# Seven products for a 2x2 block product in the attention's input projection, for sample tokens 512 to 2047

## The chip, the cores and the metric

The kernel runs on one core of a Trainium2 chip. The metric is the device time of one execution in microseconds (us). A core has these engines: PE does the matmuls (PEld, its weight loads, are listed apart), DVE, ACT and POOL work on rows of elements, and SP mostly starts DMA transfers. Each engine runs its own instructions in order and waits on semaphores for the others.

## The reference, cut to what matters

The program is one inference step of a two-layer network on 256 prompt tokens and 2048 sample tokens of 1024 channels. Layer 0 is a convolution branch. Layer 1 is an attention: the 2048 sample tokens form a grid of 32 rows and 64 columns, and each reads a neighbourhood of 8 rows and 16 columns and 512 cached context keys. The change lies in the projection that feeds it:

```
def na_project(h, w_in):                       # w_in: 1024 x 4096
    B, L, _ = h.shape
    q, k, v, z = jnp.split(h @ w_in, 4, axis=-1)
    heads = lambda t: t.reshape(B, L, N_HEADS, HEAD_DIM)    # 16 heads of 64
    return heads(q), heads(k), heads(v), z
...
        q, k, v, z = na_project(h, na_w_in[j])
        att = neighbourhood_attention(q, k, v, cache_k[:, j], cache_v[:, j], na_rpb[j])
        out = (att * jax.nn.silu(z)) @ na_w_out[j]
```

Here `h` is the normalized and modulated input of the layer. The inputs are float32. `na_rpb` is a table of biases per head, which the kernel turns into one masked bias table per head and kind of query row.

## The kernel before, in words

**Arithmetic.** Each float32 operand of a matmul is held as two rounded numbers, a high part (`h`, `hi`) and the remainder (`l`, `lo`). A product is three matmuls into the same PSUM bank: high by high, high by remainder, and remainder by high (lines L362 to L364 in `project`, L1009 to L1011 in `na_values`). The high part is a copy by ACT or a rounding by POOL (L107, `round_pool`); the remainder is a subtraction by POOL (L110, `rest_pool`) or DVE (L113, `rest_dve`). For weights, `halves` copies the high part on ACT (L354) and subtracts on POOL.

**Stages.** To some 720 us runs the convolution layer, whose order was written out by hand for all engines. Its output projection follows (`conv_out_pipeline`, `conv_out`), and the attention's input projection begins at 847 us beside its end. The attention over the sample tokens (`sa_...` tiles) begins near 1820 us, in an order written out for PE and DVE; the output projection (`o`) and the final norm end the program. Where no order is written by hand, a scheduler orders each engine's instructions from the program's order and from `high_priority` blocks. Most DMAs are issued by SP, in one queue, in order.

**The input projection.** It is done twice, for two sets of token blocks: A is the prompt, sample tokens 0 to 511 and 512 to 767; B is 768 to 1023, 1024 to 1535 and 1536 to 2047. For keys, queries and gate (`na_rest`, tiles `ni_...`), 128 output channels (one `ct` of eight) of one part (1 keys, 0 queries, 3 gate) stand as weights in PE, and a block of 256 or 512 tokens streams by, in eight steps of 128 input channels. A weight of 128 by 1024 (`nis_..._w`, or `nip_...` for A) is loaded and split for each of the 24 pairs of `ct` and part. For values (`na_values`, tiles `v_ps`), 128 tokens stand in PE and 256 channels of a weight (`wv_..._w`) stream by. A key is copied by ACT and its remainder is subtracted by DVE from PSUM; a query is scaled by ACT (L1056), then rounded and subtracted by POOL; the gate goes through a Silu on ACT (L1047). The results go to DRAM (`ks_d`, `qh_d`, `ql_d`, `zn_d`, `vs_d`) and are read back by the attention.

**Side work.** `weave(main, side, n)` steps through a main generator and, after each of its steps, `n` steps of a side generator. Beside values and rest of B are woven: the context keys (`context_keys`), the masked bias tables (`masked_bias`, DVE subtractions at L1106 into tiles `bm`, 48 stores to `bm_d`), the output weights times the gate (`gated_weights`, L1218), the context values, the prompt's own attention (`pa_...`), and its output projection (`po_...`). The last `ct` of B makes gate, keys, queries in this order, and between its last query products stand the scores of the attention's first two units (`begun`, lines L1616 and L1617). After them the attention transposes its probabilities on PE (L1649), splits them on ACT (L1658) and DVE (L113, tiles `sa_pt`), and multiplies them by the values (L1673, L1678).

The weave of set B reads:

```
side = itertools.chain(self.context_keys(), self.masked_bias())
self.weave(self.na_values(B, lambda: next(rest)), side, 2)
self.weave(itertools.islice(rest, 13), side, 3.6)
...
side = itertools.chain(self.gated_weights(), self.context_values())
side = self.mixed(self.prompt_attention(pq, pps), side, 24 / 52)
self.weave(itertools.islice(rest, 6), side, 13)
```

## Time and profile before

| what | value |
|---|---|
| runs | 2801.69, 2802.99 (median), 2808.65 us |
| the profiled execution's own time, and its span | 2800.95 us, 2799.2 us |
| granted PE clock, mean over the span | 0.988 |
| POOL busy | 1394.4 us (50%) |
| ACT busy | 1377.2 us (49%) |
| DMA queue of SP: share of 16 engines, bytes | 60.0%, 507.75 MB |

The span is what the profiler recorded from the first to the last instruction. A busy time adds up the instructions of one engine; two engines that are busy at once both count. In rows of groups of instructions, "x384" is the number of instructions, then stand the busy time and the mean ns of one, then the idle time of the engine just before them and what ended it. Names of tiles stand as out<-in, and sizes as partitions by elements.

### The profile page before, as it was taken

Reading aid. Unit: us, or ns where it says so; the run is one execution under the profiler, and the core shown is the slowest. Engines: PE = TensorE matmul, PEld = TensorE weight load, DVE = VectorE, ACT = ScalarE, POOL = GpSimd, SP = SyncE. Lnnn points to the kernel's source line nnn. Section 1 sums busy time; section 2 is a strip of 40 time slices with the busy share of each in tenths; the row PEclk is TensorE's granted clock in tenths of the full one; section 3 lists DMA queues with packets and bytes.
Section 4 is the critical chain, followed back from the end, with each engine's and each line's share of the span. In section 5 each row is a group of like instructions: output and inputs, shape, how many; then the busy total and the mean of one; then the engine's idle time right before and its main releaser. Section 6 shows DMA issues by size and latency. Waiting matters only on the chain. (4 is left out here: it accounts for less than half of the span.)

```text
span 2799.2 us, 45249 instructions
## 1 busy us (share of the span) xinstructions
PE 2685.2 (96%) x16081; PEld 2324.7 (83%) x16081; DVE 1768.4 (63%) x3052; ACT 1377.2 (49%) x2437; POOL 1394.4 (50%) x1571
## 2 busy tenths in 40 slices
PE   6999999999999999999999999978999999999998
PEld 4888877776777889999998888867888898888887
DVE  4678778888986510012556532468787787778885
ACT  4446454456453312234222244256676676666774
POOL 4687776566563343355124235134455555555564
PEclk9999999999999999999999999999999999999999
DMA  7233554555546554446889986588666767966652
GB/s 258 69 129 114 178 193 142 163 190 194 176 119 180 159 163 129 127 148 201 248 298 342 367 243 197 177 218 220 201 199 197 202 171 205 270 181 198 196 165 102
DMA packets 446490, 533.86 MB, mean 191 GB/s; under 512 B 79793, under 2 KB 322569, under 8 KB 446136
## 3 DMA queue, kind: packets, MB, share of 16 engines
q1 hardware_dynamic: 439792, 507.75, 60.0%
q10 hardware_dynamic: 6184, 22.16, 2.0%
q8 instruction: 128, 2.10, 0.3%
q0 software_dynamic: 288, 1.05, 0.1%
q14 instruction: 98, 0.80, 0.1%
HBM read 355.14 MB, written 179.79 MB: 191 GB/s over the span
## 5 line engine op out<-in xcount | busy, mean ns | idle before, releaser
L1643 POOL TENSOR_SCALAR sa_p<-sa_p,sa_m 128x992 f32<-128x992 f32 (+2 forms) x256 | 277.4, 1084 | 438.2 <-DVE sa_m L1642 299.9
L514 POOL TENSOR_TENSOR cv_p<-cv_p,cv_p 128x640 f32<-128x640 f32 (+1 forms) x240 | 358.9, 1495 | 120.8 <-ACT cv_p L511 107.9
L1658 ACT CAST sa_pt<-sa_T 128x512 fp32r<-128x512 f32 (+3 forms) x512 | 275.1, 588 | 211.6 <-PE sa_T L1649 194.4
L113 DVE TENSOR_TENSOR sa_pt<-sa_T,sa_pt 128x512 fp32r<-128x512 f32 (+3 forms) x512 | 328.4, 682 | 17.7 <-DMA a_qh<-qh_d 11.8
L362 PE MATMUL ci_ps<-h_s_hi,ci_wh 128*128 128x512 f32 x768 | 308.5, 402 | 7.6 <-ACT z L481 3.7
L363 PE MATMUL ci_ps<-h_s_lo,ci_wh 128*128 128x512 f32 x768 | 304.0, 396 | 0.0
L364 PE MATMUL ci_ps<-h_s_hi,ci_wl 128*128 128x512 f32 x768 | 303.8, 396 | 0.0
L1641 ACT ACTIVATE sa_p<-sa_S,sa_m 128x992 f32<-128x992 f32 (+2 forms) x256 | 267.1, 1043 | 67.5 <-DVE sa_m L1637 60.5
L1649 PE MATMUL sa_T<-ident,sa_p 128*128 128x128 f32 (+3 forms) x2048 | 273.3, 276 | 22.6 <-DVE sa_pt L113 22.5
L1649 PEld LDWEIGHTS sa_T<-ident,sa_p 128*128 128x128 f32 (+3 forms) x2048 | 238.0, 138 | 59.9 <-issue 14.7
L1635 DVE TENSOR_REDUCE sa_m<-sa_S 128x1 f32<-128x512 f32 x256 | 176.2, 688 | 144.9 <-PE sa_S L1617 124.9
L511 ACT ACTIVATE cv_p<-u,ws 128x640 f32<-128x640 f32 (+1 forms) x256 | 190.8, 777 | 134.1 <-DVE u L478 98.5
L534 DVE SCALAR_TENSOR_TENSOR cv<-u,dw,cv 128x640 f32<-128x640 f32 (+1 forms) x240 | 196.0, 816 | 0.5
L1678 PE MATMUL sa_O<-sa_pt,a_v 120*128 120x256 f32 (+5 forms) x1280 | 190.4, 279 | 0.0
L362 PEld LDWEIGHTS ci_ps<-h_s_hi,ci_wh 128*128 128x128 f32 x768 | 146.2, 190 | 47.6 <-ACT z L481 6.9
L534 DVE SCALAR_TENSOR_TENSOR cv<-cv_d,dw,cv 128x640 f32<-128x640 f32 (+1 forms) x224 | 182.6, 815 | 0.0
L1673 PE MATMUL sa_O<-sa_pt,cv 128*128 128x256 f32 x1024 | 175.3, 293 | 5.0 <-ACT sa_pt L1658 1.0
L1637 DVE CUSTOM_DVE_ANT_0 sa_S<-sa_S,a_bm,sa_m 128x480 f32<-128x480 f32 (+2 forms) x256 | 170.9, 667 | 12.9 <-DMA a_bm<-bm_d 4.0
L364 PEld LDWEIGHTS ci_ps<-h_s_hi,ci_wl 128*128 128x128 f32 x768 | 145.8, 190 | 34.0
L363 PEld LDWEIGHTS ci_ps<-h_s_lo,ci_wh 128*128 128x128 f32 x768 | 146.0, 190 | 31.1
L1678 PEld LDWEIGHTS sa_O<-sa_pt,a_v 120*128 120x128 f32 (+2 forms) x1280 | 167.1, 191 | 0.0
L362 PE MATMUL ni_s<-h_s_hi,nis_wh 128*128 128x512 f32 x384 | 150.1, 391 | 0.7 <-ACT ni_s_f L1047 0.7
(803 smaller groups left out, 7119.9 us busy)
## 6 DMA issues: line engine op xcount, KB each, us to landing
adaw<-in_ada_w SPq DMA_DIRECT2D x24, 1024.0 KB
ci_w<-in_conv_w_in SPq DMA_DIRECT2D x48, 512.0 KB
a_bm<-bm_d SPq DMA_DIRECT2D x32, 720.0 KB
x_s<-in_x_sample SPq DMA_DIRECT2D x32, 512.0 KB
vs_d<-v_s SPq DMA_DIRECT2D x128, 128.0 KB
a_qh<-qh_d SPq DMA_DIRECT2D x128, 128.0 KB
a_ql<-ql_d SPq DMA_DIRECT2D x128, 128.0 KB
a_v<-vs_d SPq DMA_DIRECT2D x32, 480.0 KB
```

The source lines that it names most:

```text
L113: self.nc.vector.tensor_tensor(out=lo, in0=src, in1=hi.bitcast(F32), op=ALU.subtract)
L362: self.nc.tensor.matmul(out, wh[:, k, :], hh[:, k, :], start=k == 0, stop=False)
L363: self.nc.tensor.matmul(out, wh[:, k, :], hl[:, k, :], start=False, stop=False)
L364: self.nc.tensor.matmul(out, wl[:, k, :], hh[:, k, :], start=False, stop=k == NK - 1)
L511: nc.scalar.activation(t, st["u"][:, 0, j : j + nh], AF.Copy, scale=self.ws[:, ct, j : j + 1])
L514: nc.gpsimd.tensor_tensor(out=st["t", 0], in0=st["t", 0], in1=st["t", j], op=ALU.add)
L534: nc.vector.scalar_tensor_tensor(out=st["acc", b], in0=d, scalar=w, in1=st["acc", b], op0=ALU.mult, op1=ALU.add)
L1641: nc.scalar.activation(p[:, n], S[:, n], AF.Exp, scale=-1.0, bias=m[:, 2:3], accum_out=m[:, 3:4])
L1643: nc.gpsimd.tensor_scalar(out=p[:, n], in0=p[:, n], scalar1=m[:, 3:4], scalar2=1.0, op0=ALU.mult, op1=ALU.mult)
L1649: nc.tensor.transpose(t[:w, c * P : c * P + P], p[:, x + c * w : x + c * w + w], self.ident)
L1658: nc.scalar.copy(pt[:w, 0, part, :, at], t)
L1678: nc.tensor.matmul(dst, v[:w, c0 + c].rearrange("p s d -> p (s d)"), loc[:, lo:hi], start=False, stop=s == 1 and c == 3)
```

## The change

Sample tokens 512 to 2047 leave the sets A and B. They form two sets of 768 tokens, B (512 to 1279) and C (1280 to 2047), each of two halves of 384. Set A keeps the prompt and tokens 0 to 511 and goes through the old code. For B and C the product of inputs and weights is taken as a product of 2x2 blocks: two halves of the tokens, two halves of the 1024 input channels, and two neighbouring groups of output channels (two `ct`, or two times 256 channels for values). By the rule of Strassen in Winograd's form it takes seven block products where eight are usual, of sums of blocks.

- `input_sums` makes seven input factors from four blocks and splits each into high part and remainder (tiles `hb`). C's are written into the buffers of B's.
- `weight_sums` loads the raw weights of a group, makes four sums on DVE (L1029), copies the high parts of seven factors on ACT and subtracts the remainders on POOL (L119), one to three of them on DVE (L122). `in_turn` makes them up to seven products ahead of PE.
- `rest_group` issues a product of 4 x 3 matmuls of 384 columns; `value_group` one of 3 x 4 x 3 matmuls of 256 columns. `combine` keeps two products by ACT, joins five others from PSUM on DVE (L1122) and adds twice on POOL (L1135, L1141); `rest_out` and `store_values` split and store the four results.
- The order: values of B (2 groups), keys, queries and gate of B (12 groups), of C (12), values of C (2), then the attention. Context keys, gated weights and context values stand beside B; the inputs of C and the prompt's attention beside late B and early C; the prompt's output projection beside late C.
- The masked bias tables move ahead of B, beside the end of layer 0's output projection and the rest of A, with masks in bf16 and 144 stores of one piece each.
- The first scores no longer stand among the last products. `first_loads` loads the first two heads ahead of C's last ten value products. In the last stage stores go out on ACT's and POOL's own queues (`out_queue`).

```
+HALF_SET = 384
+FACTORS = "11", "T1", "T2", "22", "T3", "21", "T4"
+AHEAD = 7
+EARLY_HEADS = 16
...
+    def input_sums(self, t0, res):
...
+            (b11, b21), (b12, b22) = both
...
+            split("11", b11, True)
+            minus(b11, b12, b11)
+            split("T1", b11, False)
+            minus(b12, b22, b12)
+            split("T3", b12, True)
+            yield
+            split("22", b22, False)
+            minus(b22, b22, b11)
+            split("T2", b22, True)
+            split("21", b21, False)
+            minus(b21, b21, b22)
+            split("T4", b21, True)
...
+    def weight_sums(self, srcs, shape, pool, nm):
...
+        def split(x, dve):
...
+            with self.tc.high_priority():
+                nc.scalar.copy(hi, x)
+                (self.rest_dve if dve else self.rest_pool)(lo, x, hi)
+            return hi, lo
+
+        yield split(a11, False)
+        s1 = tt(0, a21, a22, ALU.add)
+        yield split(s1, False)
+        s2 = tt(1, s1, a11)
+        yield split(s2, n > 512)
+        s4 = tt(2, a12, s2)
+        yield split(s4, True)
+        s3 = tt(3, a11, a21)
+        yield split(s3, n > 512)
+        yield split(a12, False)
+        yield split(a22, False)
...
+    def rest_group(self, t0, h, pair, part, pool):
...
+            pm = self.product_bank(f"{nm}_{i}")[:, :n]
+            wh, wl = w
+            hh, hl = (h[FACTORS[i]][:, s] for s in range(2))
+            for k in range(4):
+                nc.tensor.matmul(pm, wh[:, k, :], hh[:, k, :], start=k == 0, stop=False)
+                nc.tensor.matmul(pm, wh[:, k, :], hl[:, k, :], start=False, stop=False)
+                nc.tensor.matmul(pm, wl[:, k, :], hh[:, k, :], start=False, stop=k == 3)
...
+    def combine(self, i, pm, kept, tile, put, scale=None):
...
+        with self.tc.high_priority():
+            if i == 0:
+                keep("s1")
+            elif i == 1:
+                keep("s5")
+            elif i == 2:
+                t = kept["u2"] = tile("u2")
+                join(t, kept["s1"])
+                u4 = kept["u4"] = tile("u4")
+                nc.gpsimd.tensor_tensor(out=u4, in0=t, in1=kept["s5"], op=ALU.add)
+            elif i == 3:
+                join(kept["u4"], kept["u4"])
+            elif i == 4:
+                u3 = kept["u2"]
+                join(u3, u3)
+                nc.gpsimd.tensor_tensor(out=kept["s5"], in0=kept["s5"], in1=u3, op=ALU.add)
...
+            side = self.input_sums(512, B)
...
+            groups = [*self.value_sums(B, [self.xp, raws]), *self.rest_sums(B, raws), *self.rest_sums(C, raws)]
+            products = self.in_turn(groups)
...
+            self.start_attention()
+            with ExitStack() as s:
+                banks(s, "pm4", 3)
+                self.ws = s.enter_context(right("wv2"))
+                products = self.in_turn(self.value_sums(C, [self.xp, self.xp]))
+                for _ in range(4):
+                    next(products)
+                self.tail = True
+                self.first_loads()
+                for _ in products:
+                    pass
-            self.start_attention()
-            self.s0 = c.enter_context(tc.tile_pool(name="s0", bufs=1, space=bass.MemoryType.PSUM))
-            with tc.manual_schedule(engines={E.PE}):
...
-                for j in range(2):
-                    next(rest)
-                    self.begun.append(self.sample_unit(self.sequence[0], j))
-                    for _ in range(3):
-                        next(self.begun[j])
```

Three places show how the instructions stand. The first is DVE in the middle of the projection. Before, beside the prompt's attention (`pa_...`), it subtracts remainders of probabilities and keys from PSUM (`ni_1_s_l`):

```order
L113 TENSOR_TENSOR pa_pt<-pa_T_16039,pa_pt 128x512
L113 TENSOR_TENSOR pa_pt<-pa_T_16040,pa_pt 128x512
L1336 TENSOR_TENSOR pa_of<-pa_O,pa_t 64x256
L113 TENSOR_TENSOR ni_1_s_l<-ni_1_s_16060,ni_1_s_h 128x512
L1337 TENSOR_TENSOR pa_z<-pa_of,pa_z 128x256
L113 TENSOR_TENSOR ni_1_s_l<-ni_1_s_16093,ni_1_s_h 128x512
L113 TENSOR_TENSOR ni_1_s_l<-ni_1_s_16126,ni_1_s_h 128x256
```

Now, in the groups of pair 1 of set B (`ng_1_0` is its queries; `r` is a raw weight, `s` at L1029 a sum of weights, `w` a split factor, `u` and `s` at L1122 kept products; `w_30` and the like are the gated weights beside it):

```order
L1122 SCALAR_TENSOR_TENSOR ng_1_0_u_13001<-ng_1_0_2_12988,ng_1_0_s_12957 128x384
L122 TENSOR_TENSOR ng_1_3_w<-ng_1_3_s_13039,ng_1_3_w 128x512
L122 TENSOR_TENSOR w_30_12605<-w_30_12605 128x512
L122 TENSOR_TENSOR ng_1_1_10_l<-ng_1_1_u_12800,ng_1_1_10_h 128x384
L122 TENSOR_TENSOR w_31_12633<-w_31_12633 128x512
L1122 SCALAR_TENSOR_TENSOR ng_1_0_u_13003<-ng_1_0_3_13015,ng_1_0_u_13003 128x384
L1122 SCALAR_TENSOR_TENSOR ng_1_0_u_13001<-ng_1_0_4_13044,ng_1_0_u_13001 128x384
L1029 TENSOR_TENSOR ng_2_1_s_13176<-ng_2_1_r_13131 128x512
L1029 TENSOR_TENSOR ng_2_1_s_13222<-ng_2_1_r_13129,ng_2_1_r_13131 128x512
L1029 TENSOR_TENSOR ng_2_1_s_13176<-ng_2_1_s_13176,ng_2_1_r_13129 128x512
L1122 SCALAR_TENSOR_TENSOR ng_1_0_s_12957<-ng_1_0_5_13077,ng_1_0_s_12957 128x384
L1029 TENSOR_TENSOR ng_2_1_s_13222<-ng_2_1_r_13129,ng_2_1_s_13176 128x512
```

DVE now joins products and sums weights of a later group between the joins, and most of these operations have two inputs in SBUF. The second place is POOL, in the same stretch. Before, it stands with one remainder per weight and the rounding and remainder of each query block:

```order
L110 TENSOR_TENSOR nis_2_1_wl<-nis_2_1_w,nis_2_1_wh 128x1024
L110 TENSOR_TENSOR nis_2_0_wl<-nis_2_0_w,nis_2_0_wh 128x1024
L107 TENSOR_SCALAR ni_0_s_h<-ni_0_s_f 128x512
L110 TENSOR_TENSOR nis_2_3_wl<-nis_2_3_w,nis_2_3_wh 128x1024
L110 TENSOR_TENSOR ni_0_s_l<-ni_0_s_f,ni_0_s_h 128x512
```

Now, from the last keys' factor of pair 1 to its gate's first (sets of names as for DVE):

```order
L119 TENSOR_TENSOR ng_1_1_w<-ng_1_1_r_12568,ng_1_1_w 128x512
L119 TENSOR_TENSOR ng_1_0_w<-ng_1_0_r_12737,ng_1_0_w 128x512
L119 TENSOR_TENSOR ng_1_0_w<-ng_1_0_s_12782,ng_1_0_w 128x512
L1135 TENSOR_TENSOR ng_1_1_u_12802<-ng_1_1_u_12800,ng_1_1_s_12780 128x384
L119 TENSOR_TENSOR ng_1_0_w<-ng_1_0_s_12782,ng_1_0_w 128x512
L119 TENSOR_TENSOR ng_1_0_w<-ng_1_0_s_12844,ng_1_0_w 128x512
L119 TENSOR_TENSOR ng_1_0_w<-ng_1_0_r_12737,ng_1_0_w 128x512
L1141 TENSOR_TENSOR ng_1_1_s_12780<-ng_1_1_s_12780,ng_1_1_u_12800 128x384
L119 TENSOR_TENSOR ng_1_0_w<-ng_1_0_r_12739,ng_1_0_w 128x512
L119 TENSOR_TENSOR ng_1_3_w<-ng_1_3_r_12940,ng_1_3_w 128x512
```

Six factor remainders per group have come, with two additions of kept products between them. The third place is PE at the change to the attention. Before, the last query product (`ni_0_s`) stands ahead of unit 2's scores, the scores of units 0 and 1 (`sa_0_0_S`, `sa_0_1_S`) being earlier:

```order
L363 MATMUL ni_0_s_17076<-h_s_hl,nis_7_0_wh 128x256
L364 MATMUL ni_0_s_17076<-h_s_hl,nis_7_0_wl 128x256
L1616 MATMUL sa_0_2_S<-ck_16758,a_0_qh 128x512
L1617 MATMUL sa_0_2_S<-ck_16758,a_0_ql 128x512
L1616 MATMUL sa_0_2_S<-a_0_k,a_0_qh 128x352
L1617 MATMUL sa_0_2_S<-a_0_k,a_0_ql 128x352
L1649 MATMUL sa_0_0_T_17132<-ident,sa_0_0_p 128x128 x4
```

Now the last value product of set C (`vg_1_6`) stands there:

```order
L1210 MATMUL vg_1_6_17937<-vg_1_wl,hb_T_13354 128x256
L1211 MATMUL vg_1_6_17937<-vg_1_wh,hb_T_13354 128x256
L1933 MATMUL sa_0_0_S<-ck_17424,a_0_qh 128x512
L1934 MATMUL sa_0_0_S<-ck_17424,a_0_ql 128x512
...
L1933 MATMUL sa_0_2_S<-a_0_k,a_0_qh 128x352
L1934 MATMUL sa_0_2_S<-a_0_k,a_0_ql 128x352
L1966 MATMUL sa_0_0_T_18043<-ident,sa_0_0_p 128x128 x4
```

All scores of the first units now follow the last product of the projection, and three units' scores stand ahead of the first transposes.

More of the change, by code (lines that the diff above doesn't have):

```diff
@@ new lines, in in_turn, with load @@
+    def in_turn(self, groups):
+        todo = [(g, i) for g in groups for i in range(7)]
+        made, loaded, live = [], 0, 0
+        def load(upto):
+            nonlocal loaded
+            while loaded < min(upto, len(groups)):
+                next(groups[loaded]["w"])
+                loaded += 1
+        load(1)
+        for at, (g, i) in enumerate(todo):
+            while len(made) < len(todo):
+                j = len(made)
+                cost = todo[j][0]["cost"]
+                if j > at and live + cost > self.ahead:
+                    break
+                load(j // 7 + 1)
+                made.append(next(todo[j][0]["w"]))
+                live += cost
+                if j % 7 == 6:
+                    load(j // 7 + 2)
+            w, made[at] = made[at], None
+            g["product"](i, w)
+            live -= g["cost"]
+            yield
@@ L1397, in phase1 @@
             out = self.conv_out(w, rest, ready)
-            self.weave(self.na_rest(A), out, 2)
-            prep = itertools.chain(out, *(self.layer1_block(*b, B) for b in rest[1:]))
-            self.weave(self.na_values(A, lambda: None), prep, 2)
-            for _ in itertools.chain(prep, self.layer1_block(*rest[0], B)):
+            own = self.na_rest(A)
+            with tc.tile_pool(name="mb", bufs=1, side="right") as self.mb:
+                side = self.mixed(out, self.masked_bias(range(EARLY_HEADS), 4, self.xp), EARLY_HEADS / 12)
+                self.weave(itertools.islice(own, 16), side, (12 + EARLY_HEADS) / 15.5)
+                for _ in side:
+                    pass
@@ new lines, in phase1 @@
+                prompt = c.enter_context(ExitStack())
+                pq = prompt.enter_context(tc.tile_pool(name="pq", bufs=2))
+                pqs = prompt.enter_context(tc.tile_pool(name="pqs", bufs=1, space=bass.MemoryType.PSUM, side="right"))
+                pa = map(bool, self.prompt_attention(pq, pqs))
+                self.ahead = AHEAD - 3
+                ahead = self.input_sums(1280, C)
+                self.weave(more(32), ahead, 0.4)
+                self.weave(more(10), self.mixed(ahead, pa, 1), 1.2)
@@ L1419, in phase1 @@
+                for _ in ahead:
+                    pass
+                self.weave(more(42), pa, 2)
+                for _ in pa:
+                    pass
+                self.ahead = AHEAD
+                prompt.close()
+                with tc.tile_pool(name="po", bufs=1) as po, tc.tile_pool(name="pops", bufs=1, space=bass.MemoryType.PSUM, side="right") as pps:
+                    side = self.prompt_out(po, pps)
+                    self.weave(more(42), side, 2)
                     for _ in side:
```

450 lines of the change are left out of this document (303 added, 147 removed).

## The prediction

> **What bounds the kernel now.** I read the busy times first, then a table of windows over the stretch that the change rewrites (847 to 1860 us, from the first projection product to the start of the attention), then the matmul rows there, then the waits.
>
> ```profile
> PE 2685.2 (96%) x16081; PEld 2324.7 (83%) x16081; DVE 1768.4 (63%) x3052; ACT 1377.2 (49%) x2437; POOL 1394.4 (50%) x1571
> GB/s 258 69 129 114 178 193 142 163 190 194 176 119 180 159 163 129 127 148 201 248 298 342 367 243 197 177 218 220 201 199 197 202 171 205 270 181 198 196 165 102
> ```
> ```profile
> core 0: us, PE busy (x) PEld busy (x) DVE busy (x) ACT busy (x) POOL busy (x), PEclk, DMA share, GB/s
> 847.00:1240.00 393.00, 387.24 (x2364) 342.22 (x2363) 100.47 (x125) 106.76 (x198) 153.06 (x135) 1.00 0.51 148
> 1240.00:1345.00 105.00, 102.97 (x880) 102.75 (x879) 41.47 (x80) 45.99 (x93) 57.91 (x81) 1.00 0.64 212
> 1345.00:1442.00 97.00, 93.60 (x785) 92.78 (x784) 46.21 (x81) 21.53 (x45) 14.85 (x6) 1.00 0.85 269
> 1442.00:1700.00 258.00, 253.81 (x1375) 220.01 (x1374) 130.10 (x186) 85.51 (x173) 93.04 (x86) 1.00 0.93 308
> 1700.00:1800.00 100.00, 99.25 (x524) 85.03 (x524) 37.35 (x61) 34.66 (x63) 25.51 (x30) 1.00 0.51 161
> 1800.00:1860.00 60.00, 44.97 (x261) 38.64 (x260) 24.65 (x57) 21.71 (x41) 15.14 (x18) 0.89 0.81 219
> ```
>
> PE is the bound: of the 953 us from 847 to 1800 it is idle 16 (the five differences of length and PE busy), while DVE and POOL are busy 355 and 344 us. Only the last window, the change to the attention, loses much (15 us). "Busy" could still hide slow matmuls, so the second look is at starts:
>
> ```profile
> 1500.10 0.39 PE L362 MATMUL ni_s<-h_s_hi,nis_wh 128*128 128x512 f32 x1
> ...
> 1505.54 0.39 PE L362 MATMUL ni_s<-h_s_hi,nis_wh 128*128 128x512 f32 x1
> ```
> ```profile
> 1300.01 0.28 PE L1009 MATMUL v_ps_p<-wv_p_wh,h_p_hl 128*128 128x256 f32 x1
> ...
> 1303.90 0.28 PE L1009 MATMUL v_ps_s<-wv_p_wh,h_s_hi 128*128 128x256 f32 x1
> ```
>
> Between the first pair lie 24 steps: 5.44/24 = 0.2267 us per matmul of 512 columns. Between the second lie 33: 3.89/33 = 0.1179 us per 256. The 0.39 and 0.28 are latencies that overlap.
>
> **Step 1, fewer products.** The matmuls of tokens 512 to 2047, one of three equal lines each:
>
> ```profile
> L362 PE MATMUL ni_s<-h_s_hi,nis_wh 128*128 128x512 f32 x384 | 150.1, 391 | 0.7 <-ACT ni_s_f L1047 0.7
> L362 PE MATMUL ni_s<-h_s_hl,nis_wh 128*128 128x256 f32 x192 | 54.0, 281 | 1.1 <-ACT ni_s_f L1056 1.1
> L362 PE MATMUL ni_s<-h_s_hl,nip_wh 128*128 128x256 f32 x192 | 53.5, 279 | 0.6 <-POOL h_s_hl L107 0.6
> L1009 PE MATMUL v_ps_s<-wv_s_wh,h_s_hi 128*128 128x256 f32 x256 | 72.5, 285 | 0.0
> ```
>
> Keys, queries and gate: 1152 of 512 columns (261.2 us) and 1152 of 256 (135.8). Values: 12 token tiles x 4 x 24 = 1152 of 256 (135.8). Sum 532.8. Afterwards: 24 groups x 7 products x 12 = 2016 of 384 columns, and 4 x 7 x 36 = 1008 of 256 (118.8). No row has 384 columns in such a stream; halfway between the two rates is 0.1723, so 347.4. Bounds: 512's rate per column gives 0.170 (342.7), 256's gives 0.177 (356.6). New sum 466.2: **-66.6 us** (-57 to -71). The weight loads stay hidden, since 256 columns already hide one in the rows above. The 256 tokens that leave the first pass move at the same price and are in the sum.
>
> **Step 2, the sums and splits, and the port they share.** Per group of keys, queries or gate (84 products' matmuls, 14.5 us of PE): ACT copies 7 factors, DVE makes 4 sums and one remainder, POOL six remainders; DVE then does five joins from PSUM, POOL two additions, and the outputs are split. Rows:
>
> ```profile
> L110 POOL TENSOR_TENSOR ni_s_l<-ni_s_f,ni_s_h 128x512 fp32r<-128x512 f32 x24 | 31.9, 1331 | 9.7 <-DMA ks_d<-ni_s_h 4.5 <-DMA ks_d<-ni_s_l 2.1 <-DVE bm L1106 1.8
> L110 POOL TENSOR_TENSOR ni_s_l<-ni_s_f,ni_s_h 128x256 fp32r<-128x256 f32 x16 | 11.9, 745 | 10.6 <-DMA qh_d<-ni_s_h 9.2 <-DMA ql_d<-ni_s_l 0.4
> L1312 POOL TENSOR_SCALAR pa_p<-pa_p,pa_m 128x256 f32<-128x256 f32 x32 | 15.4, 498 | 11.5 <-DVE pa_m L1310 11.5
> L1218 DVE TENSOR_TENSOR po_t<-po_raw,po_gate 128x512 f32<-128x512 f32 x16 | 11.0, 691 | 18.8 <-DMA po_raw<-in_na_w_out 18.5
> L113 DVE TENSOR_TENSOR v_s<-v_ps_s,v_s 128x256 fp32r<-128x256 f32 x64 | 26.7, 419 | 94.9 <-ACT v_s L1083 73.0 <-DMA vp_d<-v_p 20.9 <-DMA vs_d<-v_s 1.0
> L1154 ACT CAST ni_s_h<-ni_s 128x512 fp32r<-128x512 f32 x22 | 12.9, 586 | 59.9 <-PE ni_s L364 42.9 <-DMA vs_d<-v_s 8.5 <-DMA ql_d<-ni_s_l 8.3
> ```
>
> By interpolation 384 columns cost 1.04 us on POOL and 0.55 on DVE, 128 cost 0.45 on POOL. Each engine alone fits in the 24 groups' time of about 391 us (347.4 of products, and 43 of prompt attention, prompt output and transposes beside them: 128 matmuls of 256 columns, 96 of 512, 112 transposes at an estimated 0.06). POOL: 144 x 1.33 + 48 x 1.04 + 36 for the queries' remainders + 15.9 + about 30 of norms, rounds and prompt remainders = 323. ACT: 24 x about 7 us (7 x 0.59 and six outputs near 0.48) = 168 and the side work. DVE: about 285. But they are not independent:
>
> ```profile
> 1540.92 1.40 DVE L1106 TENSOR_TENSOR bm<-mask,rb 128x352 f32<-128x352 f32 x3 [1.49 <-DMA bm_d<-bm]
> 1508.06 3.60 DVE L1106 TENSOR_TENSOR bm<-mask,rb 128x352 f32<-128x352 f32 x3
> 1544.91 2.46 DVE L1106 TENSOR_TENSOR bm<-mask,rb 128x480 f32<-128x480 f32 x1 [0.69 <-DMA bm_d<-bm]
> 1506.22 0.68 DVE L113 TENSOR_TENSOR ni_s_l<-ni_s,ni_s_h 128x512 fp32r<-128x512 f32 x1
> ```
> ```profile
> 1508.32 2.52 POOL L110 TENSOR_TENSOR nis_wl<-nis_w,nis_wh 128x1024 fp32r<-128x1024 f32 x1 [8.29 <-ACT nis_wh L354]
> 1544.47 2.39 POOL L110 TENSOR_TENSOR nis_wl<-nis_w,nis_wh 128x1024 fp32r<-128x1024 f32 x1 [6.19 <-ACT nis_wh L354]
> ```
>
> Three bias subtractions take 1.40 us with POOL at rest and 3.60 beside one POOL subtraction; the single one that began inside POOL's 2.39 us ended 0.51 us after POOL did. So a DVE operation whose two inputs both lie in SBUF and POOL's operations take turns. In the new stretch DVE has 224 of these: 120 in the groups, 33 in the second set's input sums and 39 of side work (512 columns), and 32 key remainders (384 columns, from SBUF now; before they read PSUM). That is 192 x 0.69 + 32 x 0.55 = 150 us, and 323 + 150 = 473 is 82 more than PE's 391. That upper end counts tails that overlap: back to back a 512 starts every 0.61 us (below), and POOL alone takes 2.39, not the 2.5 beside DVE; with both, 132 + 306 = 438, and the pair of rows above shows 1.40 + 2.39 = 3.79 alone in 3.60, 0.95 of it: 416, or **+25 us**, which I take as the observed pair. The lower end is 0, if POOL's gaps hold the sums.
>
> ```profile
> 1505.61 0.69 DVE L1218 TENSOR_TENSOR w_41t<-w,gate 128x512 f32<-128x512 f32 x1 [0.51 <-DMA w_d<-w_31h]
> ```
>
> The Trainium skill ("SBUF — State Buffer", section "Who interferes with whom") states that a DVE instruction with two SBUF inputs and a GpSimd instruction that reads SBUF exclude each other for the whole instruction; the 1544.91 row agrees. By that rule the sum would take the 82, which is the third rival below.
>
> **Step 3, the change to the attention.** Before, the first heads' scores stand between the last query products, and then:
>
> ```profile
> PE sa_T L1649 <- DVE sa_pt L113: 22.5, 18, 12.3
> ACT sa_pt L1658 <- DMA ql_d<-ni_s_l: 10.0, 1, 10.0
> ```
> ```profile
> L1083 ACT CAST v_s<-v_ps_s 128x256 fp32r<-128x256 f32 x64 | 23.4, 370 | 71.9 <-PE v_ps_s L1011 43.7 <-DMA vs_d<-v_s 28.2
> ```
>
> PE waits 12.3 us in one piece, because the buffer of the first probabilities is freed by the last queries' stores. Now the values come last and their stores go out on ACT's queue. What is late next is ACT: three casts (370 ns each as in a values tile), their six stores, the exponent's table and the first exponent; with the last join (an estimated 0.95 on DVE) and POOL's scaling I estimate 9 us of idle PE: **-3 us** (-12 if ACT is free at once, +6 if its queue holds the first exponent further).
>
> **Step 4, what is moved.** The bias tables go to 847 to 1170:
>
> ```profile
> L1106 DVE TENSOR_TENSOR bm<-mask,rb 128x480 f32<-128x480 f32 x48 | 38.6, 857 | 21.1 <-DMA bm_d<-bm 21.1
> L1106 DVE TENSOR_TENSOR bm<-mask,rb 128x352 f32<-128x352 f32 x48 | 37.0, 822 | 35.8 <-DMA bm_d<-bm 24.0 <-DMA rb<-rpb_d 6.8 <-issue 4.9
> L1106 DVE TENSOR_TENSOR bm<-mask,rb 128x384 f32<-128x384 f32 x48 | 30.3, 684 | 4.1 <-DMA bm_d<-bm 4.1
> ```
>
> They are 106 us of DVE and 61 of waiting, beside some 100 already there, in about 325 us of PE (393 less the 68 that moves away): hidden, with the queries' and keys' evictions of DVE behind them. SP issues 144 stores for 48 (two thirds more at a time, the same bytes); the weights are read and split for three token sets instead of two, which the groups' count holds. New hand-overs (PSUM banks re-cut twice; the second set's inputs written into the first's buffers while its last group still reads them): **+6 us**, estimated from the 16 us that all of this stretch's hand-overs cost now (0 to 16).
>
> Sum: -66.6 + 25 - 3 + 6 = **-38.6**. The profiled execution took 2800.95 us (span 2799.2), 2 below the median of the runs, so 2762 for it and 2765 for the median.
>
> **Rivals.** (a) The port costs nothing because DVE's sums fall into POOL's gaps; for it, POOL is far from full beside PE and seven factors are made ahead; against it, 438 of 391. Time 2801 - 66.6 - 3 + 6 + 2 = 2739. (b) The transfers become the bound in the six groups beside the context work: 6 MB of weights, 8 of outputs and some 19 of gated weights and context values in 87 us are 380 GB/s, and no slice of the page is above 367; at the 308 of the 1442 window it takes 107 us, 20 more, and with SP's issue order behind it 25: 2790. Against it, PE hardly waits in that window now, at a DMA share of 0.93. (c) The port is exclusive in full and the joins queue behind it in order, so PSUM banks come late: 82 in place of 25, 2822, slower. It decides at 72 (463 us of port time): there the gain is back to a loss of 0.3%.
>
> **How the numbers follow.** My case 0.47 (its own range 2752 to 2786, by half and by one and a half port prices and step 1's bounds); (a) 0.25; (b) 0.15; (c) 0.13. Differences under 0.3% (8.4 us) can't be told from no change. Faster: 0.47 + 0.25 + half of (b) = 0.80; same: the rest of (b), 0.07; slower: (c), 0.13. The range goes from just under (a) to short of (c): 2736 to 2815.
>
> **What would show it.** Step 1: 2016 matmuls of 384 columns, 0.172 us apart. Step 2: DVE sums of 512 columns with a mean over 1.0 us where 0.69 is the free price, POOL near 0.8 busy in these 390 us, and PE waits that name POOL's or DVE's factor remainders, 25 us in all. Step 3: one PE wait near 9 us before the first transposes. Step 4: PE idle under 8 us from 847 to the first value product. I am wrong if the factors' remainders are never waited for (a), if the waits name weight loads (b), or if the waits exceed 70 us (c).

## The result: 2942 us in place of 2802, 4.9% slower

The changed kernel takes 2942.07 us (median of four runs, 2939.64 to 2947.43) against 2802.34 for the kernel before: a ratio of 1.0494 [1.0469, 1.0518]. I had said 2765, with 0.13 on "slower". The profiled execution is the longest of the four (2947.43, span 2945.6). I read it as I read the first one. The busy row and the clock row of its page:

```profile
PE 2697.3 (92%) x15649; PEld 2349.5 (80%) x15649; DVE 2097.5 (71%) x3375; ACT 1514.6 (51%) x2739; POOL 1650.6 (56%) x1715
...
PEclk9999999999999999899979899999999999999999
```

PE runs 432 matmuls fewer and is busy 12 us *longer*; DVE and POOL have 329 and 256 us more to do. The windows say where. Columns: the stretch, its length, busy time and instructions of each engine, granted clock, DMA share, GB/s. First before, from the first product of layer 0's output projection to the last matmuls of 512 columns of the attention's input projection (24 of 256 columns, 2.8 us, follow behind the cut at 1821.70), then the change to the attention and the attention:

```profile
715.10:1821.70 1106.60, 1081.85 (x6600) 960.54 (x6599) 471.84 (x672) 362.63 (x699) 413.43 (x416) 1.00 0.66 205
1821.70:1842.00 20.30, 7.50 (x50) 6.59 (x49) 4.29 (x11) 4.19 (x8) 4.73 (x6) 0.76 0.91 248
1842.00:2760.00 918.00, 890.08 (x5988) 793.90 (x5988) 739.57 (x1623) 632.08 (x1154) 490.61 (x703) 0.99 0.70 198
```

Then after: the same stretch up to its last matmul, most of its pieces in order of time, and the same two pieces behind it:

```profile
723.70:1965.30 1241.60, 1085.60 (x6189) 983.83 (x6187) 796.82 (x984) 496.20 (x995) 669.95 (x563) 0.94 0.67 198
818.30:1215.50 397.20, 358.09 (x1804) 297.27 (x1803) 242.79 (x299) 119.61 (x225) 162.57 (x133) 0.96 0.74 226
1215.50:1304.00 88.50, 75.38 (x593) 73.51 (x592) 32.58 (x39) 29.11 (x58) 47.80 (x40) 0.90 0.42 136
1304.00:1381.30 77.30, 65.25 (x536) 64.44 (x534) 44.39 (x54) 28.93 (x52) 31.85 (x17) 0.95 0.57 174
1381.30:1528.30 147.00, 114.69 (x604) 111.62 (x604) 101.29 (x121) 57.50 (x113) 82.66 (x62) 0.88 0.85 251
1528.30:1700.00 171.70, 136.59 (x730) 129.94 (x731) 116.66 (x142) 96.33 (x222) 133.65 (x125) 0.87 0.56 158
1700.00:1803.50 103.50, 96.03 (x567) 93.26 (x566) 74.55 (x103) 59.07 (x131) 85.48 (x83) 0.98 0.79 221
1803.50:1897.40 93.90, 88.28 (x458) 80.36 (x458) 69.81 (x82) 39.23 (x78) 61.47 (x50) 1.00 0.65 181
...
1965.30:1990.00 24.70, 7.53 (x31) 6.16 (x30) 8.79 (x22) 7.59 (x15) 1.98 (x3) 0.67 0.56 148
1990.00:2908.00 918.00, 889.92 (x5987) 793.41 (x5987) 739.50 (x1623) 632.65 (x1154) 491.85 (x703) 1.00 0.70 199
```

The attention itself is untouched (918.0 both times). The projection's stretch grows by 135.0 us. PE is idle 156.0 us of it where it was idle 24.8: **+131.3**. PE is busy 3.7 longer, although the matmuls of step 1 have gone. At the full pace of the rows in the prediction (0.2267 and 0.1179 us for 512 and 256 columns) and, now measured, 0.1732 for 384 (41 steps from 1456.71 to 1463.81 us), step 1's sum goes from 532.8 to 349.2 + 118.8 = 468.0: **-64.8**, near the forecast of -66.6. Of the matmuls whose records lie in the two stretches it is -62.5, mainly since the cut leaves 2.8 us of the projection out of the first. Counted in this way, with the transposes, the first stretch holds some 1055 us of matmuls at full pace and the second some 993; PE's busy time is 27 and 93 over that. So the matmuls that stayed are **+66** us slower. With 4.4 at the change to the attention, 8.6 ahead of the stretch (same instructions; not looked into) and -1.6 in the tail, the 135.0 make the 146.4 between the spans.

Why matmuls get slower is seen in PE's timeline behind a short and behind a longer wait (start, latency, instruction, in brackets the idle time before it and what ended it):

```profile
1456.46 0.41 PE L1100 MATMUL ng<-hb_T,ng_w 128*128 128x384 f32 x1 [1.62 <-DVE ng_u L1124]
1456.71 0.33 PE L1101 MATMUL ng<-hb_T,ng_w 128*128 128x384 f32 x1
1456.88 0.34 PE L1102 MATMUL ng<-hb_T,ng_w 128*128 128x384 f32 x1
...
1490.38 0.69 PE L1100 MATMUL ng<-hb_T,ng_w 128*128 128x384 f32 x1 [4.57 <-DVE ng_u L1124]
1490.87 0.52 PE L1101 MATMUL ng<-hb_T,ng_w 128*128 128x384 f32 x1
1491.18 0.52 PE L1102 MATMUL ng<-hb_T,ng_w 128*128 128x384 f32 x1
...
1495.84 0.34 PE L1100 MATMUL ng<-hb_T,ng_w 128*128 128x384 f32 x1
1496.01 0.34 PE L1101 MATMUL ng<-hb_T,ng_w 128*128 128x384 f32 x1
```

After 1.62 us of idling the next matmuls start 0.17 apart, from the second on. After 4.57 us they start 0.31 to 0.32 apart, for 5.5 us, and then 0.17 again: the clock column's 0.87 and 0.88 in the two windows with the longest waits. The trace of the changed kernel has 19 windows in this stretch in which the granted clock is 0.50. Their sum, and PE's busy time in them:

```profile
sum 156.98, PE 99.72 PEld 89.28 DVE 89.25 ACT 47.19 POOL 68.80; mean PE 5.25 PEld 4.70 DVE 4.70 ACT 2.48 POOL 3.62
```

Before, such windows were 6.8 us, with PE busy in all of them. At half the pace half of the busy time is lost, 49.9 us of it now and 3.4 before: some **46** of the 66 us are the half clock. The other 20 are lost at the full clock and were not looked into; a part goes with the restarts (72 idle gaps of more than 0.2 us where there were 25, and the first start above comes 0.25 ahead of the second in place of 0.17). A wait need not be as long as 4.57 us for it: the clock is 0.50 as well behind a wait of 3.25 us (to 1092.35) and one of 2.58 us (to 1673.10), and for 13.7 us from 843.86 about three waits of 2.25, 1.53 and 1.40 us. The waits themselves over the whole execution (total, times, longest):

```profile
PE pa_S L1933 <- DMA pa_ql<-ql_d: 20.3, 1, 20.3
PE hb_t L970 <- POOL x1r_s L276: 20.0, 4, 9.3
PE sa_S L1933 <- ACT sa_p L1958: 14.8, 1, 14.8
PE ng L1100 <- DVE ng_u L1124: 12.1, 6, 4.6
...
PE ni_p L366 <- POOL nip_wl L119: 9.5, 5, 2.9
```

No one cause carries the 131 us: loads of the prompt's attention (`pa_...`), norms of the inputs (`hb_t`), joins (`ng_u`), split weights (`nip_wl`); the 14.8 of `sa_S` lies behind the stretch. So I took the change apart.

### The profile page after: what moved, and what is told of

The parts are those of the page before. It is cut to its first block, busy times and chain, and to the rows that moved or that the text cites. A ratio compares the mean times of both kernels' runs of the same rounds, so it can differ in the third digit from the quotient of the medians.

```text
span 2945.6 us, 45787 instructions
## 1 busy us (share of the span) xinstructions
PE 2697.3 (92%) x15649; PEld 2349.5 (80%) x15649; DVE 2097.5 (71%) x3375; ACT 1514.6 (51%) x2739; POOL 1650.6 (56%) x1715
## 3 DMA queue, kind: packets, MB, share of 16 engines
q0 software_dynamic: 288, 1.05, 0.1%
## 5 line engine op out<-in xcount | busy, mean ns | idle before, releaser
L122 DVE TENSOR_TENSOR sa_pt<-sa_T,sa_pt 128x512 fp32r<-128x512 f32 (+3 forms) x512 | 328.4, 683 | 3.7 <-ACT sa_pt L1975 3.6
L366 PEld LDWEIGHTS ci_ps<-h_s_hi,ci_wl 128*128 128x128 f32 x768 | 146.4, 191 | 35.6
L1365 DVE TENSOR_TENSOR bm<-masks,rb 128x352 f32<-128x352 bf16 (+2 forms) x144 | 114.2, 830 | 70.0 <-DMA bm_d<-bm 54.5
```

The costliest lines, as they stand in the source:

```text
L122: self.nc.vector.tensor_tensor(out=lo, in0=src, in1=hi.bitcast(F32), op=ALU.subtract)
L366: self.nc.tensor.matmul(out, wl[:, k, :], hh[:, k, :], start=False, stop=k == NK - 1)
```

## The experiments

Every ratio is against the kernel before on the same chip. To compare them I give each as us over 2800, that is 2800 x (ratio - 1): the changed kernel stands at +138. The expectations name two theories. By P, POOL and DVE are late because of the port they share; by M, the side work that was moved, and the hand-overs, hold up the engines that serve PE.

**The helpers' load: sums, remainders and the port.** Four kernels change what DVE and POOL do for the seven factors. First, no sums of weights on DVE:

```diff
-            t = temps(i)
-            nc.vector.tensor_tensor(out=t, in0=x, in1=y, op=op)
-            return t
+            return x
```

> Left out: the four sums of weight blocks of each group (a raw block stands in for each), 112 DVE operations of some 1.2 us; the seven factors are still copied and their remainders still made. Theory P: DVE has 130 us less to do, and POOL is no longer held by it, so most of the waits on joins and factors go: 60 us or more less than 2942. Theory M: the large waits stand at hand-overs (the prompt attention's loads, the inputs of the last set, the bias tables), so 10 to 25 less.

Measured 2907.93 against 2798.44, 1.0392 [1.0369, 1.0415]: +110, so the sums cost 28. Second, no factor remainders on POOL:

```diff
-                (self.rest_dve if dve else self.rest_pool)(lo, x, hi)
-            return hi, lo
+                if dve:
+                    self.rest_dve(lo, x, hi)
+            return hi, lo if dve else hi
```

> Left out: the remainders of the weight factors that POOL makes (the third matmul of a product takes the high part again), 158 operations and some 250 us of POOL; the sums on DVE stay. Theory P: DVE's sums go back from 1.2 us to about 0.69 each and POOL is free, 60 us or more less than 2942. Theory M: less than 25 less.

Measured 2883.41, 1.0307 [1.0275, 1.0340]: +86, so they cost 52, the largest single item. Third, POOL still writes each of these tiles but reads nothing:

```diff
-                (self.rest_dve if dve else self.rest_pool)(lo, x, hi)
+                if dve:
+                    self.rest_dve(lo, x, hi)
+                else:
+                    nc.gpsimd.memset(lo.bitcast(F32), 0.0)
```

> Left out: the remainders of the weight factors that POOL makes; POOL writes zeros into the same tiles instead and reads nothing. Leaving POOL's operation out altogether gave 2883. If it was the shared port, DVE's sums of 512 columns fall from 1.2 to about 0.7 us although POOL still works, and the time is 2880 to 2895; if it was POOL's own queue being late, the time stays near 2920 to 2940 in proportion to POOL's busy time.

Measured 2890.24 against 2800.73, 1.0324 [1.0277, 1.0371]: +91, not told apart from the second. DVE's sums of 512 columns from 1300 to 1970 us (count, then minimum, median and maximum in ns), in the changed kernel and then with POOL only writing:

```profile
L1029 DVE TENSOR_TENSOR ng_s<-ng_s,ng_r x24: 675/1385/1782, 1369.2 to 1857.3; 128x512 f32<-128x512 f32 x24
L1029 DVE TENSOR_TENSOR ng_s<-ng_r,ng_s x24: 676/1318/1780, 1370.0 to 1860.5; 128x512 f32<-128x512 f32 x24
```
```profile
L1029 DVE TENSOR_TENSOR ng_s<-ng_s,ng_r x24: 671/684/1510, 1357.9 to 1816.8; 128x512 f32<-128x512 f32 x24
L1029 DVE TENSOR_TENSOR ng_s<-ng_r,ng_s x24: 673/684/911, 1360.2 to 1819.9; 128x512 f32<-128x512 f32 x24
```
```profile
L1042 POOL MEMSET ng_w<- 128x512 f32 x144 | 74.1, 526 | 94.9 <-PE ng L1105 79.6 <-PE vg L1213 7.1 <-ACT hb L985 3.1
```

144 writes of 526 ns leave these sums at their free price of 0.684 in the median; beside POOL's subtractions these two kinds take twice that (the other two kinds of sums have medians of 0.936 and 0.896 there). The Trainium skill ("SBUF — State Buffer", section "Who interferes with whom") says that a GpSimd instruction that only writes does not contend; these rows agree. But POOL's own time for the remainders fell from 218 us (two kinds of 72 subtractions, 1558 and 1491 ns each) to 74 as well, so how much of the 47 is the port and how much POOL's length is not told apart. Fourth, two factors' remainders of a group go from POOL to DVE:

```diff
-        yield split(s2, n > 512)
+        yield split(s2, True)
...
-        yield split(s3, n > 512)
+        yield split(s3, True)
```

> Nothing left out. Of the six factor remainders of a key, query or gate group that POOL makes, two (of the second and the fourth weight sum) go to DVE, 48 in all: POOL 48 x 1.5 = 72 us less, DVE 48 x 0.7 more. Theory P: the port is taken for 72 us less and 33 more, so some 15 to 25 less than 2942. Theory M: DVE is the later of the two (its joins and evictions queue behind), so no change or up to 15 more.

Measured 2930.61, 1.0458 [1.0417, 1.0500]: +128, whose interval overlaps that of the change. To share this load otherwise gains little alone; to have less of it gains more.

**The bias tables.** One head's table is made in place of sixteen:

```diff
+            if h:
+                for _ in range(3):
+                    yield
+                continue
...
-        nc.sync.dma_start(hd.bm[:, :, :nl], self.bm_d[h, GKIND[G]][:, :, :nl])
+        nc.sync.dma_start(hd.bm[:, :, :nl], self.bm_d[0, GKIND[G]][:, :, :nl])
```

> Left out: the masked bias tables of 15 of the 16 heads (every head reads the first head's). All else as in the changed kernel, whose PE stands idle 150.6 us between 818 and 1965 us, 52 of it before 1304 where the tables were moved to. Theory M (the moved and handed-over side work holds up the engines that serve PE): DVE no longer stands 70 us behind the tables' stores and loads there, the idle time before 1304 falls from 52 to about 17 and the slow matmuls after waits by some 18 more, so 2942 falls by 45 to 60, to about 2890. Theory P (POOL and DVE are late because of the shared port, in the groups of seven products): less than 15 less.

Measured 2922.00, 1.0438 [1.0409, 1.0467]: +123. In the trace the stretch beside which the tables stand shrinks more (the same products; the changed kernel first, then one table):

```profile
818.30:1227.90 409.60, 360.54 (x1814) 298.88 (x1812) 250.07 (x307) 122.73 (x231) 168.95 (x140) 0.95 0.72 222
```
```profile
810.50:1192.00 381.50, 354.16 (x1814) 295.90 (x1812) 146.98 (x172) 122.70 (x231) 160.56 (x140) 0.97 0.53 155
```

28 us there (409.60 to 381.50), about half of which is lost again later. The edit leaves out the tables' loads and stores too (DMA share 0.72 to 0.53), so how much of it is DVE's work in the way is not told apart. How a table stops PE, in the changed kernel's timeline:

```profile
1086.05 5.64 DVE L1365 TENSOR_TENSOR bm<-masks,rb 128x352 f32<-128x352 bf16 x5 [4.14 <-DMA bm_d<-bm]
...
1091.61 0.68 DVE L826 TENSOR_TENSOR co_os<-co_s,gate 128x512 f32<-128x512 f32 x1
...
1092.35 0.50 PE L364 MATMUL ni_s<-h_s_hi,nip_wh 128*128 128x512 f32 x1 [3.25 <-DVE co_os L826]
```

DVE stands still 4.14 us because earlier tables are still being stored, then does five subtractions in 5.64, and only then empties the bank that PE wants. The page counts 54.5 us of DVE idling before these subtractions for the stores:

```profile
L1365 DVE TENSOR_TENSOR bm<-masks,rb 128x352 f32<-128x352 bf16 (+2 forms) x144 | 114.2, 830 | 70.0 <-DMA bm_d<-bm 54.5
```

If SP's queue were what holds the stores, ACT's would be sooner:

```diff
-                    nc.sync.dma_start(self.bm_d[h, gk, :, i, : 32 * R], t[:, : 32 * R])
+                    nc.scalar.dma_start(self.bm_d[h, gk, :, i, : 32 * R], t[:, : 32 * R])
```

> Nothing left out. The 144 stores of the masked bias tables are issued by ACT instead of SP. If DVE's 54 us of waits for these stores come from SP's queue (other transfers' waits ahead of them), they fall by half and the time by 10 to 15 from 2942; if they come from the transfers themselves with four buffers, nothing changes or ACT's own waits add up to 10.

Measured 2941.52, 1.0503 [1.0463, 1.0542]: +141, no change, and DVE's idling for these stores is 50.5 us in place of 54.5. It is not SP's issue.

**The order in PE's queue.** At 1528 us PE waits for the prompt's scores, which stand ahead of products of the projection in its queue (that these were ready is not shown):

```profile
1528.35 0.55 PE L1933 MATMUL pa_S<-pa_k,pa_qh 128*128 128x256 f32 x1 [20.30 <-DMA pa_ql<-ql_d]
1541.40 0.55 PE L1933 MATMUL pa_S<-pa_k,pa_qh 128*128 128x256 f32 x1 [7.76 <-DMA pa_qh<-qh_d]
1547.60 1.97 PE L970 MATMUL hb_t<-ident,x1r_s 128*128 128x128 f32 x8 [5.65 <-POOL x1r_s L276]
```

Some 36 us of idling, with half-pace work between. The DMA engines are nearly full in this time, so the loads may be slow as well as late:

```profile
1512.87:1550.41 37.54, 6.12 (x22) 5.03 (x23) 9.61 (x17) 12.00 (x26) 5.03 (x8) 0.50 0.93 300
```

Two kernels move what stands there: the side work beside B goes sooner, and then the prompt's attention goes behind C's inputs as well (its first head made to wait for their last tile):

```diff
-                    self.weave(more(42), side, 0.65)
+                    self.weave(more(42), side, 1.0)
```

> Nothing left out; the gated weights and context values are woven beside set B's groups at 1.0 steps per product in place of 0.65, so that they end before the 42 products and not after them, where PE stood idle 36 us between 1507 and 1548. Theory M: 15 to 35 less than 2942. Theory P: DVE is busy 20 of 20 us in that stretch, so the same work only comes earlier and the waits move: no change, or up to 10 more.

Measured 2931.17, 1.0475 [1.0453, 1.0496]: +133, not clearly different.

```diff
+                self.weave(more(42), ahead, 0.45)
+                for _ in ahead:
+                    pass
...
+                self.made = C[1]["T4"][:, 1, 3, HALF_SET - 1 : HALF_SET]
...
-                self.weave(more(32), ahead, 0.4)
-                self.weave(more(10), self.mixed(ahead, pa, 1), 1.2)
...
+        if ct == 0:
+            nc.vector.tensor_copy(k[:, 0, 0:1], self.made)
```

> Nothing left out. On top of the sooner side work (2931): the prompt's attention is begun only when the input factors of the last set are made (a copy of one of their elements into the first key tile holds its load back), so that PE no longer meets its first scores ahead of set B's products. Theory M (PE stands at moved steps whose place in its queue was chosen too early): the 22 us of waits between 1509 and 1534 go, and some 3 to 5 of slow matmuls behind them: 20 to 28 less than 2931. Theory P (POOL and DVE are late through the shared port): the same products then wait for their factors, less than 8 less.

Measured 2961.45, 1.0572 [1.0533, 1.0610]: +160, slower still. My theory that this order is the cause of the hole fell. The prompt's wait goes, and others open:

```profile
1413.53 0.69 PE L1100 MATMUL ng<-hb,ng_w 128*128 128x384 f32 x1 [11.37 <-ACT ng_w L1038]
...
1530.83 1.97 PE L970 MATMUL hb_t<-ident,x1r_s 128*128 128x128 f32 x8 [22.18 <-POOL x1r_s L276]
```

**What a wait costs.** To price waits without the change I put twelve into the kernel before: after every third product of the last set POOL rewrites one column of the inputs, which the next product has to wait for, at once or behind six more operations.

```diff
+        nc.scalar.activation(zero, pm[:, 0:1], AF.Copy, scale=0.0)
...
+            for _ in range(0):      # 6 in the second kernel
+                nc.gpsimd.tensor_scalar(out=scr, in0=scr, scalar1=zero, scalar2=1.0, op0=ALU.mult, op1=ALU.mult)
+            for i, (src, t0, n, hi, lo) in enumerate(blocks):
+                nc.gpsimd.tensor_tensor(out=hi[:, 0, 0:1], in0=self.kept[:, i : i + 1], in1=last, op=ALU.add)
```

> The kernel before, with 12 waits of PE put into its keys, queries and gate of set B: after every third product the next one waits until ACT has read a column of its result and POOL has rewritten one input column of each block (three operations of one column). Nothing left out. Each wait should be some 1.3 us. Theory C (a wait of more than some 2.5 us is followed by about 5 us at half the pace, a shorter one is not): 12 x 1.3 = 16 us more than before, PE's busy time unchanged. The rival, that a wait costs its own length whatever it is: the same 16.

> As the short waits, with six POOL operations of 256 columns in the chain, so that each of the 12 waits is about 4 us. Theory C: 12 x 4 of waiting and 12 x 2.5 of slow matmuls, some 75 to 80 us more than before, and PE's busy time up by about 30 with the same matmuls. The rival: 48 us more and PE's busy time as it was.

The waits, and the window of the second half of this projection, first with none and then with six:

```profile
PE ni_s L363 <- POOL h_s_hi L1027: 52.8, 12, 17.3
1440.00:1800.00 360.00, 307.17 (x1537) 262.18 (x1536) 132.62 (x201) 98.38 (x210) 109.67 (x133) 0.89 0.72 234
```
```profile
PE ni_s L363 <- POOL h_s_hi L1027: 113.9, 12, 25.7
1440.00:1800.00 360.00, 245.02 (x1157) 206.55 (x1156) 109.72 (x162) 68.78 (x140) 128.60 (x169) 0.81 0.61 201
```

Measured 2878.65 and 2938.71 against 2798.38: 1.0282 [1.0251, 1.0312] and 1.0498 [1.0475, 1.0522], that is 80.3 and 140.3 us. I missed the lengths: even with nothing in between, ten of the twelve waits last 3.6 us or more (one 17.3), so the first kernel is not the short case that I wanted, and a kernel with short waits alone was not run. But the pair prices the long ones. Beyond its own length the time grows by 27.5 us for ten long waits and by 26.4 for eleven, 2.7 and 2.4 each, though the second kind are twice as long: what a long wait adds here is a toll of about 2.5 us that does not grow with its length. It lies in the matmuls behind the wait: over the whole execution, with the same 16081 matmuls, PE is busy 2716.3 and 2709.6 us where it was busy 2685.2. The granted clock is 0.50 behind every one of these long waits, for another 5.2 to 6.1 us in the first kernel and 3.1 to 5.7 in the second, half of which is 2.8 and 2.5 us on average. The Trainium skill ("TensorE: Matmul & The Clock Gate", section "What's actually happening") gives the mechanism: after an idle window of about 3.4 us the array runs at half its clock until it has been busy for as long. The waits from 3.6 us up agree; that shorter ones have it too is seen above (2.58 us). The toll here is more than the 1.7 us that 3.4 us at half pace would cost (an estimate from that page), since the half pace lasted 5.5 us in the rows of 1490 and 5.2 us or more in the first of these kernels.

**Cures and combinations.** Two moves that alone were not told apart from the change, two remainders to DVE and side work sooner, together with a third: the norms of B's and C's inputs two tiles ahead of their transposes.

```diff
+        xts = [norm(a) for a in at[:ahead]]       # ahead = 2
...
+                if i + ahead < len(at):
+                    xts.append(norm(at[i + ahead]))
+                xt = xts[i]
```

> Nothing left out. Three changes to the changed kernel together: two more remainders of each group on DVE (alone 2931), side work woven sooner (alone 2931), and the load and norm of the last sets' input tiles two tiles ahead of their transposes. If the savings add up and the 20 us of waits for normalized inputs go too, with what follows them, 2890 to 2905; if DVE is the one that is late by now, 2915 to 2930.

Measured 2900.96, 1.0366 [1.0341, 1.0390]: +102. This is the best version that computes everything, clearly better than the change and still 3.7% slower than before. The waits for normed inputs (`hb_t` on `x1r_s`) shrink from 20.0 to 4.7 us, and a new one stands in the groups:

```profile
1402.08 0.69 PE L1112 MATMUL ng<-hb,ng_w 128*128 128x384 f32 x1 [12.37 <-ACT ng_w L1050]
```
```profile
1401.40 0.62 ACT L1050 CAST ng_w<-ng_r 128x512 fp32r<-128x512 f32 x1 [1.75 <-DMA ng_r<-in_na_w_in]
```

The raw weights came late: SP issued their load at 1396.07. Three kernels tried to have them sooner: the loads on POOL's queue, in the change and in the kernel of three cures, and there two kinds of side stores on ACT's queue instead of SP's.

```diff
-            nc.sync.dma_start(flat, src)
+            nc.gpsimd.dma_start(flat, src)
```

> Nothing left out. The loads of raw weight blocks are issued by POOL instead of SP, all else as in the changed kernel. If SP's queue holds these loads back, the 7.6 and 12.7 us of ACT and DVE waits for raw weights go and the time falls by 10 to 20 from 2942; if POOL, which is late itself, issues them no earlier, no change or up to 15 more.

> Nothing left out. The three cures of 2901 together with the loads of raw weights on POOL's queue. There PE waits 12.4 and 8.6 us for copies of raw weights whose loads were issued at the last moment: without them, with the slow matmuls behind each, 2875 to 2885; if POOL issues them as late, 2895 to 2915.

```diff
-                nc.sync.dma_start(self.cvs_d[u * P : u * P + P, hs], v.bitcast(F32))
+                nc.scalar.dma_start(self.cvs_d[u * P : u * P + P, hs], v.bitcast(F32))
...        (and both w2_d stores)
```

> Nothing left out. The three cures of 2901, and the 40 stores of the gated weights and the context values are issued by ACT in place of SP. If the raw weights' loads came late because they stood behind these stores in SP's queue, the waits of 12.4 and 8.6 us for copies of raw weights shrink to under 4 and the time to 2875 to 2890. If ACT, which makes those copies itself, now waits for DVE's remainders before it can issue, the waits stay and the time is 2900 to 2920.

Measured 2988.28 (1.0667 [1.0625, 1.0709]), 2930.07 (1.0490 [1.0449, 1.0531]) and 2917.42 (1.0425 [1.0398, 1.0453]): +187, +137 and +119, all worse than without. On POOL's queue the loads stand behind POOL's own waits:

```profile
POOL pa_p L1578 <- DMA pa_qh<-qh_d: 38.7, 1, 38.7
```

The edit also moves these loads from the queue that the page calls hardware_dynamic to the one it calls software_dynamic (34.61 MB there in place of 1.05), and which of the two matters was not tried. Where all of the 49 us of the first comes from, and why the raw loads come late at all, stays open. Last, the three relieved loads together (no sums, no POOL remainders, one table), and then with sooner side work, earlier norms and the raw weights on POOL's queue:

> Left out together: 15 heads' bias tables, the weight sums, and POOL's remainders of weight factors (alone 2922, 2908 and 2883). If the helpers' load is what the loss comes from, the three add up apart from an overlap of the last two: 2810 to 2845. If hand-overs and the order in PE's queue make up the rest, it stays at 2855 to 2875.

> Left out as before in the run of 2847: 15 heads' bias tables, the weight sums, POOL's remainders of weight factors. Added: side work sooner, input tiles normed ahead, raw weights on POOL's queue. If load of the helpers, SP's queue and the order around the last set's inputs together make the loss, 2795 to 2815, where PE's own work and some 70 us of other waits with their slow matmuls remain; if the order in PE's queue is another cause, 2830 or more.

Measured 2846.96 (1.0168 [1.0143, 1.0194]) and 2829.11 (1.0116 [1.0087, 1.0145]): +47 and +32. Singly the three gave 28, 52 and 15, together 91 where the sum is 95: they hardly share anything. The same stretch in these two:

```profile
716.70:1867.90 1151.20, 1055.15 (x6189) 963.99 (x6187) 512.32 (x740) 498.41 (x998) 396.12 (x402) 0.96 0.64 186
```
```profile
717.60:1849.70 1132.10, 1052.67 (x6189) 965.10 (x6187) 520.63 (x740) 498.54 (x999) 450.85 (x467) 0.97 0.64 189
```

Here DVE and POOL are busy about as long as before the change (512 and 396 against 472 and 413), and yet the first has 96 us of idle PE (24.8 before) and 63 of slower matmuls (27 before, each over the full pace as counted above). The largest waits of this kernel in the stretch are the ones that the order in PE's queue could matter for:

```profile
PE pa_S L1936 <- DMA pa_v<-vp_d: 18.4, 1, 18.4
...
PE ng L1099 <- ACT ng_w L1036: 12.8, 6, 8.7
...
PE hb_t L970 <- POOL x1r_s L276: 9.6, 2, 5.8
PE pa_S L1936 <- DMA pa_qh<-qh_d: 8.8, 3, 7.3
```

## Why the prediction was wrong, by its steps

**Step 1 was right.** 2016 matmuls of 384 columns, 0.1732 us apart (0.1723 forecast); -64.8 at that pace (-66.6).

**Step 2 had the mechanism and not the size.** The sums' means were to be over 1.0 us; they are 1.13 to 1.29, with medians up to 1.385. POOL was to be 0.8 busy; from 1381 to 1897 it is 363 of 516 us, 0.70, of a stretch that grew. I took +25 with 82 as the upper bound. Leaving out POOL's remainders gives 47 to 52 and the sums 28: together near 80, the bound, each with the half-pace matmuls behind its waits. I weighed the engines' total time against PE's; but a total that fits does not say that each bank and each factor is ready in its turn. The waits were to name factor remainders for 25 us and do for 4 (L1102 on `ng_w`, 3.8); the waits that PE has name joins, copies and inputs instead. That these are late because they queue behind the remainders is argued from the in-order queues, not shown wait by wait.

**Step 3 was small and of the wrong sign.** One wait near 9 us: it is 14.8 (`sa_S` on ACT's `sa_p`). The idle time of the change grew by 4.4 us (17.2 of 24.7 us from 12.8 of 20.3) where I had forecast -3.

**Step 4 is the step that failed most.** From the forecast to the result are 177 us. Step 2's size is about 55 of them, steps 1 and 3 some 9; the other 113 fall on what step 4 put at "hidden" and at +6, and on the term that was missing. "Hidden" for the bias tables: they cost 15 of 2800, and 28 in their own stretch, where DVE serves its queue in order and the tables wait for stores in it. "Hand-overs +6 (0 to 16)": I took the 16 us that all hand-overs of the old stretch cost as a ceiling for the new one. PE was to be idle under 8 us up to the first value product; of the 397 us from 818 to 1215 it is idle 39, and of the whole stretch 131 more than before. That old value was the price of an order in which every helper had slack; the new one gives DVE 325 us and POOL 257 us more work in the stretch, and puts the prompt's scores and C's transposes ahead of other products in PE's queue. Which part of this order costs what stays open, as below.

**A term was missing.** Busy time of the matmuls that stay was taken as fixed. It is +66 us, as much as step 1 saves, and some 46 of that stand in windows in which the clock was halved behind waits of a few microseconds. The rows of before hardly show it (clock 1.00 in all windows but the last of the prediction's table, at 0.89), but that 0.89 with 15 us of idling was the sign.

**The rivals.** (a) is excluded by the durations of the sums. (b) is not it: in the windows of B's groups, to which it gave its 20 us, no more than 251 GB/s move, where the prediction's window from 1442 moved 308. But about the prompt's first scores (1513 to 1550) 300 GB/s move, and for those 36 us of idling it is not excluded. (c) had the right sign and the full port price, but its 2822 covers a third of the way from 2765 to 2942 (57 of 177). No rival had several small waits that together pay the toll.

**What is settled.** Neither theory came out as it was put: without the sums 28 us go, just over what M allowed and far from P's 60; without POOL's remainders 52, between the two; without the tables 15, where M said 45 to 60 and P less than 15. From -65 to +138 are 203 us. The sums, POOL's remainders and 15 tables account for 91, shown by leaving them out. Sooner side work, earlier norms and the weights on POOL's queue go with 15 more, though the two intervals just meet and that queue alone made things slower. The other 97 or so have no cause that is shown. In the last kernel most of them are idle PE (79 us of the stretch, 24.8 before) and slower matmuls (60 over the full pace, 27 before). That the order in PE's queue and its late loads make them is argued from the waits: of the moves that ran alone (side work sooner, the prompt behind C's inputs, table stores on ACT, two remainders on DVE, weights on POOL's queue) none clearly helped, and of the combinations that compute everything the one of three moves did, by 36.

## What to carry to other kernels

On an engine that is 96% busy, count what a change puts on the engines that feed it, in the order in which they serve their queues, and not their total against its total: here 65 us of matmuls were saved and 582 us of DVE and POOL work put in their place. Price a wait of 3.6 us or more on PE at its length and about 2.5 us, as here, and look in the granted clock for stages that pay it, also with shorter waits. Idle time that a tuned order shows is no ceiling for another order.

## What the runs showed of the hardware that I had not expected

- The toll: PE runs at half pace for some 5.5 us after a wait of 4.57 us and not after one of 1.62; 2.7 and 2.4 us for each long wait in two kernels built for it, whose waits were 3.6 us and longer, whatever the length. Shorter waits had it too: one of 2.58 us, and three of 2.25, 1.53 and 1.40 us close together.
- A round trip from PE's result through one column on ACT and three one-column writes on POOL back to PE kept PE idle for 3.6 to 4.0 us in nine of twelve cases (rows of 4.04, 4.03 and 4.04 among them), with no further operation of mine in the chain.
- POOL writing 512 columns takes 526 ns and leaves DVE's two-input sums at 684 ns in the median; beside POOL's subtractions of about 1.5 us the four kinds of sums have medians of 0.90 to 1.39 us.
